# Queue order of a three-branch encoder layer from a timeline simulation

## The chip, the core and the metric

The kernel runs on one core of a Trainium2 chip. The metric is the device time of one execution in microseconds, as the median of several runs. The profile and the trace come from one further execution under the hardware profiler. The engines are TensorE (PE, its weight loads PEld), VectorE (DVE), ScalarE (ACT), GpSimd (POOL) and SyncE (SP), which issues all DMAs of this kernel. Each has a queue of its own that it works off in order, and waits for other engines by semaphores.

## The reference

One layer (DEPTH = 1) on x of shape (1, 1024, 1024) in float32. All three branches read the same modulated, normalised input through one wide projection. The inner functions are only named here; each is a loop over 1024 tokens or over chunks of them.

```python
mod = silu(c) @ ada_w + ada_b                       # shift, scale, gate
h = rmsnorm(x, pre_g) * (1.0 + scale) + shift
proj = h @ w_in                                     # 1024 -> 10496 columns
a_x, a_z, b_u, b_z, c_u, c_z, g_all = split_cols(proj, ...)
y_a = mlstm_branch(a_x, a_z, ...)                   # chunked matrix memory, both directions
filt = hyena_filter(feats, t, ...)
y_b = hyena_branch(b_u, b_z, ..., filt, hy_bias)    # gated long convolution by FFT
y_c = rwkv_branch(c_u, c_z, ...)                    # 16 heads, delta rule, both directions
g_a, g_b, g_c = split(sigmoid(g_all), 3)
merged = g_a * (y_a @ w_branch_a) + g_b * (y_b @ w_branch_b) + g_c * (y_c @ w_branch_c)
x = x + gate * rmsnorm(merged @ w_out, post_g)
```

## The kernel before

Everything is float32. A projection keeps float32 accuracy by splitting both operands into a high and a low part, so each product of a 128 x 128 weight block with 512 tokens is three matmuls (gemm, L343 to L356: high by high L351, low by high L352, high by low L353) that accumulate over eight blocks in a PSUM tile pg, of which there are three. Weights come by load_w (L327 to L335): a DMA into wraw (3 buffers), a cast to wh on ScalarE (L333) and the difference wl on GpSimd (L334; 4 buffers each). ScalarE and VectorE take the result out of PSUM, with the three-tap filters of the branches on the way (taps_job, L409), and the stores to DRAM go out on SyncE.

The stages, in the order of Trunk.all (L1278): modulate (L502) makes h; then _mlstm (L574), the filter and the convolution of the Hyena branch (L870 to L1091); then rwkv (L1347), eight pairs of heads one after the other; then merge (L1142), which ends with the output projection (L1259), the norm and the residual.

The projections are not a stage of their own. Each is a generator in a list of jobs (add, L359; fill, L362), and the stages call fill between their own steps, so that in program order a few matmuls of the projections stand between the steps of a branch. In the scan this is done by weave (L72): per pair of heads, 64 steps of scan (L1740) with owed projection steps spread evenly over them, and at numbered steps the parts of the neighbouring pairs (L1401 to L1420): load, prep, the triangular solve tphase (L1597, on VectorE for the most part: tm and Tb by the helper tt, L476), bonus and post. head_sums (L1424) are two matmuls with a matrix of ones.

A chunk of the scan (L1754 to L1804) is a chain: matmuls U, copy us on VectorE (L1769), matmuls SA, copies into SV on VectorE (L1775) and ScalarE (L1776), matmuls SN, two sums on VectorE (sn), copies into SV for the next chunk on VectorE (L1800) and ScalarE (L1801). All matmuls of the chain write a PSUM tile pch. in_turn (L391) issues a row of small matmuls as a closed run: the first at L395, the others at L398, each tied behind the one before by issue_after and with the highest priority. beside (L384) ties small side work behind an instruction in the same way.

The kernel is written with a tile context. The code only traces instructions in program order; the queues are made when the context is left. Then the traced program is played on a simulated machine, and whenever an engine can take an instruction, it is given, of those whose inputs are ready in that play, the one with the earliest place in program order. tc.high_priority(n) moves the place n instructions forward (in the scan 400 for tphase), and tc.issue_after(i) fixes that what is traced inside is queued behind i on the same engine. The buffers of the pools are handed out in the same play: an instruction that needs a buffer of a pool with none free counts as not ready. The semaphore waits are put in afterwards, for the order found. So the order of each queue, SyncE's DMA issues among them, depends on the durations and delays that the simulated machine gives to each instruction, but what is computed doesn't.

## Time and profile before

| | |
|---|---|
| median of 3 runs | 2182.08 us (2180.28 to 2186.04) |
| the profiled execution | 2200.05 us, span 2198.3 us |
| DMA moved | 262.19 MB, 169384 packets, mean 119 GB/s |
| HBM read, written | 181.06 MB, 78.12 MB |
| SyncE's issues of weight blocks (wraw from w_in) | 340 of 128 KB, 2.3 us from issue to landing |
| chunks of the scan | 128 (8 pairs of 16) |

Span is the time from the first to the last instruction; what lies around it is in the time of the execution but not in the trace. Busy times are a union over an engine's instructions. A matmul's end is modelled and matmuls overlap in the pipeline, so the time from one start to the next is shorter than the duration shown, and a busy TensorE isn't TensorE at its peak. In the view of waits a row gives the idle time of an engine just before its instruction and the instruction that ended this wait.

### The profile page before, as it was taken

The page shows a single profiled execution, that of the slowest core. Times are in us where ns is not written, and L with a number is a line of the kernel's source. Part 1 is how long each engine was busy: PE and PEld are TensorE (multiplying, and loading weights), DVE is VectorE, ACT ScalarE, POOL GpSimd, SP SyncE. Part 2 cuts the span into 40 slices and gives each one's busy share as a digit, 9 for nine tenths or more (in the row PEclk, how much of TensorE's full clock was granted, in tenths as well). Part 3 has the DMA queues.
Part 4 walks back from the last instruction along what each step waited for, and adds up shares of the span by engine and source line. Part 5 has one row for each costly group of instructions (what it writes and reads, how often), then busy time and mean ns, then how long its engine had stood idle before and what let it go on. Part 6 is the DMA issues. An engine that isn't in the chain of part 4 may idle for free. (4 is left out here: it accounts for less than half of the span.)

```text
span 2198.3 us, 45984 instructions
## 1 busy us (share of the span) xinstructions
PE 1994.0 (91%) x17098; PEld 1509.2 (69%) x17098; DVE 1634.6 (74%) x4754; ACT 1103.2 (50%) x2558; POOL 424.3 (19%) x485
## 2 busy tenths in 40 slices
PE   6999899999989899899989999999898887897998
PEld 4666777787868677666766676666666665675786
DVE  4854999988447947788787888868887888764536
ACT  5557356454242115664665756667466564532221
POOL 2211311122222432311101111111114411010200
PEclk9999999999999999999998999999899998897999
DMA  8211222334465345321322333224143542445623
GB/s 255 70 67 59 78 77 90 112 101 127 143 200 172 119 138 163 124 68 61 130 79 93 117 106 102 92 81 136 52 155 118 187 144 63 159 143 175 196 89 129
DMA packets 169384, 262.19 MB, mean 119 GB/s; under 512 B 17863, under 2 KB 87335, under 8 KB 169160
## 3 DMA queue, kind: packets, MB, share of 16 engines
q1 hardware_dynamic: 169160, 259.25, 36.3%
q8 instruction: 135, 2.21, 0.4%
q14 instruction: 89, 0.73, 0.1%
HBM read 181.06 MB, written 78.12 MB: 118 GB/s over the span
## 5 line engine op out<-in xcount | busy, mean ns | idle before, releaser
L334 POOL TENSOR_TENSOR wl<-wraw,wh 128x256 fp32r<-128x256 f32 x408 | 371.5, 915 | 1488.6 <-ACT wh L333 1464.8
L351 PE MATMUL pg<-hh,wh 128*128 128x512 f32 x1440 | 601.5, 418 | 20.9 <-ACT wh L333 11.8
L352 PE MATMUL pg<-hh,wl 128*128 128x512 f32 x1440 | 594.3, 413 | 16.4 <-POOL wl L334 16.3
L353 PE MATMUL pg<-hl,wh 128*128 128x512 f32 x1440 | 592.4, 412 | 1.9 <-DVE hl L565 1.8
L351 PEld LDWEIGHTS pg<-hh,wh 128*128 128x128 f32 x1440 | 278.7, 194 | 88.9 <-ACT wh L333 15.1
L352 PEld LDWEIGHTS pg<-hh,wl 128*128 128x128 f32 x1440 | 279.3, 194 | 78.0 <-POOL wl L334 22.2
L353 PEld LDWEIGHTS pg<-hl,wh 128*128 128x128 f32 x1440 | 278.1, 193 | 62.0 <-DVE hl L565 2.8
L333 ACT CAST wh<-wraw 128x256 fp32r<-128x256 f32 x408 | 162.7, 404 | 220.6 <-PE pg L353 122.1
L476 DVE TENSOR_TENSOR tm<-Ab,Tb 128x126 f32<-128x126 f32 (+22 forms) x496 | 145.4, 293 | 4.4 <-DMA Tb<-in_tinit 2.7
L476 DVE TENSOR_TENSOR Tb<-Tb,tm 128x126 f32<-128x126 f32 (+22 forms) x496 | 144.2, 291 | 1.9
L473 DVE SCALAR_TENSOR_TENSOR st<-pg,hmu,st 128x511 f32<-128x511 f32 (+1 forms) x130 | 80.9, 636 | 27.9 <-ACT e L424 17.6
L476 DVE TENSOR_TENSOR G<-pgr,gmask 128x512 f32<-128x512 f32 x128 | 85.4, 679 | 17.0 <-PE pgr L398 17.0
L457 ACT ACTIVATE st<-pg 128x512 f32<-128x512 f32 x74 | 44.2, 597 | 99.9 <-PE pg L353 95.0
L1684 ACT COPY G<-ar 64x128 f32<-64x128 f32 x256 | 64.3, 295 | 48.4 <-DVE G L476 46.6
L473 DVE SCALAR_TENSOR_TENSOR st<-st,pg 128x512 f32<-128x512 f32 x80 | 54.3, 679 | 35.7 <-PE pg L353 12.7
L398 PE MATMUL pgr<-ar,bk 64*128 64x128 f32 x896 | 76.9, 287 | 0.0
L141 DVE SCALAR_TENSOR_TENSOR row<-row 64x1 f32<-64x1 f32 x393 | 72.7, 208 | 2.1
L1769 DVE COPY us<-pch 128x128 f32<-128x128 f32 x128 | 36.3, 283 | 45.8 <-PE pch L398 45.5
L395 PEld LDWEIGHTS pch<-SV,G 128*64 128x64 f32 x256 | 25.3, 139 | 65.5 <-ACT SV L1801 52.3
L395 PE MATMUL pch<-SV,G 128*64 128x64 f32 x256 | 43.2, 252 | 27.7 <-ACT SV L1801 26.2
L476 DVE TENSOR_TENSOR dw<-dw,dw 128x512 f32<-128x512 f32 x92 | 67.1, 760 | 0.9
L395 PEld LDWEIGHTS pch<-SV,B 128*64 128x64 f32 x256 | 25.3, 139 | 60.1 <-ACT SV L1776 50.1
(677 smaller groups left out, 4228.4 us busy)
## 6 DMA issues: line engine op xcount, KB each, us to landing
wraw<-in_w_in SPq DMA_DIRECT2D x340, 128.0 KB, 2.3
low<-lora SPq DMA_DIRECT2D x32, 512.0 KB, 4.1
sig<-st SPq DMA_DIRECT2D x48, 256.0 KB, 2.6
st<-sig SPq DMA_DIRECT2D x48, 256.0 KB, 3.5
wraw<-in_w_br SPq DMA_DIRECT2D x68, 128.0 KB, 2.8
adw<-in_ada_w SPq DMA_DIRECT2D x16, 512.0 KB, 7.1
x<-in_x SPq DMA_DIRECT2D x8, 512.0 KB, 6.1
hx<-st SPq DMA_DIRECT2D x16, 256.0 KB, 2.0
```

The lines of the kernel that those rows point to most:

```text
L141: self.ops.append(lambda: self.nc.vector.scalar_tensor_tensor(o, a, s, b, op0=op0, op1=op1))
L333: self.nc.scalar.copy(hi, raw)
L334: self.nc.gpsimd.tensor_tensor(lo, raw, hi.bitcast(F32), op=SUB)
L351: nc.tensor.matmul(p, wh, hh, start=(k == 0), stop=False)
L352: nc.tensor.matmul(p, wl, hh, start=False, stop=False)
L353: nc.tensor.matmul(p, wh, hl, start=False, stop=(k == n - 1))
L395: ins = f()
L398: ins = f()
L457: self.nc.scalar.activation(o, p, AF.Tanh, scale=0.5)
L473: return self.nc.vector.scalar_tensor_tensor(out, in0, s, in1, op0=op0, op1=op1)
L476: return self.nc.vector.tensor_tensor(out, a, b, op=op)
L1684: nc.scalar.copy(G[0:64, :, d, h, 0:64], cx["al"][g, d, b % 4][hsl[h]])
```

## The change

One argument of the tile context. The play that orders the queues runs on another simulated machine: before, on the default one, which the scheduler builds for itself; after, on a simulator of the device's timeline, which holds sequencers, queues, engines and DMA as separate resources. Nothing else of the kernel differs: the same instructions are traced, in the same program order, with the same priorities, ties and pools.

```diff
--- before.py
+++ after.py
@@ -1908,7 +1908,7 @@
     A = {n: nc.dram_tensor(f"in_{n}", a.shape, mybir.dt.from_np(a.dtype), kind="ExternalInput").ap()
          for n, a in arrays.items()}
     O = {"out": nc.dram_tensor("out_x", (T, D), F32, kind="ExternalOutput").ap()}
-    with tile.TileContext(nc) as tc:
+    with tile.TileContext(nc, schedule_with_timeline_sim=True) as tc:
         with ExitStack() as ctx:
             Trunk(ctx, tc, A, O).all()
     r = run_bass_kernel_spmd(nc, [{f"in_{n}": a for n, a in arrays.items()}], core_ids=[0])
```

## The prediction, before the result was known

> **What bounds the kernel now.** I read the first lines of the page for the busy shares, then cut the span by stage with the view of windows, then asked the view of waits stage by stage who held TensorE up, and last looked at single places in the timeline.

> ```profile
> span 2198.3 us, 45984 instructions
> PE 1994.0 (91%) x17098; PEld 1509.2 (69%) x17098; DVE 1634.6 (74%) x4754; ACT 1103.2 (50%) x2558; POOL 424.3 (19%) x485
> ...
> core 0: us, PE busy (x) PEld busy (x) DVE busy (x) ACT busy (x) POOL busy (x), PEclk, DMA share, GB/s
> 0.00:110.00 110.00, 85.78 (x459) 58.56 (x460) 72.93 (x295) 56.14 (x96) 25.02 (x27) 0.94 0.55 162
> 110.00:905.00 795.00, 742.72 (x3500) 583.77 (x3498) 597.02 (x1798) 353.41 (x787) 208.18 (x218) 0.97 0.36 118
> 905.00:1985.00 1080.00, 977.73 (x12360) 719.38 (x12360) 858.55 (x2489) 643.34 (x1583) 171.59 (x217) 0.95 0.34 109
> 1985.00:2198.30 213.30, 187.77 (x780) 147.46 (x780) 106.10 (x176) 50.29 (x94) 19.48 (x23) 0.92 0.46 152
> ```

> The four windows are the modulation of x, the mLSTM and Hyena branches, the RWKV scan with its 16 chunks in each of 8 pairs, and the merge. TensorE is the busiest engine in all four. Its idle time is the length less the first number: 24.2, 52.3, 102.3 and 25.5 us, 204.3 in all. Half of it lies in the scan, where VectorE is also busy for 858.55 of 1080 us, so neither engine is full and the time is lost in waiting on each other. Who waits there, for TensorE alone (line, what it waited for, us in total, times, longest):

> ```profile
> PE pch L395 <- ACT SV L1801: 26.2, 25, 5.4
> PE pch L395 <- ACT SV L1776: 21.0, 29, 1.7
> PE pch L395 <- DVE us L1769: 11.7, 20, 2.6
> PE plw L1552 <- DMA low<-lora: 8.3, 8, 1.6
> ```

> The first three rows are the scan's own chain: a chunk's matmuls need a copy (us, SV) that VectorE or ScalarE makes of the matmul before. The projections (the gemm, tile pg) are woven between as filling, and they depend on no chunk. One place shows why TensorE stands still all the same:

> ```profile
> 1833.74 0.39 PE L352 MATMUL pg<-hh,wl 128*128 128x512 f32 x1
> 1835.55 0.27 PE L395 MATMUL pch<-SV,G 128*64 128x64 f32 x1 [1.42 <-ACT SV L1801]
> ...
> 1836.16 0.50 PE L353 MATMUL pg<-hl,wh 128*128 128x512 f32 x1
> ```

> L351 to L353 are three products of one weight block. The third stands behind the chunk's matmul and could have run in the 1.42 us before it: its weights were in use by the matmul before, and when its turn comes it starts with no wait of its own. The queue is in order here, so the place in the queue decides. That is what the change can move; it moves nothing else.

> **What the change does to the work.** It adds and removes no instruction of the kernel: 17098 matmuls, 4754 VectorE and 2558 ScalarE instructions, and every DMA stay, so busy time at a given clock stays. Program order, the edges of issue_after and the offsets of high_priority stay as well, and with them the closed runs of matmuls:

> ```profile
> L398 PE MATMUL pgr<-ar,bk 64*128 64x128 f32 x896 | 76.9, 287 | 0.0
> L1769 DVE COPY us<-pch 128x128 f32<-128x128 f32 x128 | 36.3, 283 | 45.8 <-PE pch L398 45.5
> ```

> The 896 followers of the pgr runs have 0.0 us of idle time ahead of them; they will keep it. What moves is which ready instruction goes first on each of the five queues, SyncE's DMA issues among them, and with it which buffer of a pool frees when. The sum is made on the profiled execution, 2200.05 us (span 2198.3 and 1.75 around it), which is 1.0082 of the median of the three runs, 2182.08; a result of the sum is multiplied by 0.9918.

> Step 1, chain waits in the scan. 26.2 + 21.0 + 11.7 = 58.9 us in 74 waits, 0.80 us each. Undisturbed, the same shape of matmul starts every 87.30/384 = 0.227 us:

> ```profile
> 2102.20:2189.50 87.30, 87.30 (x384) 71.37 (x382) 44.59 (x87) 18.97 (x35) 0.00 (x0) 1.00 0.32 106
> 1854.50:1878.40 23.90, 18.21 (x276) 14.12 (x274) 17.49 (x67) 8.70 (x19) 0.72 (x1) 0.50 0.13 45
> ```

> So a mean wait holds three matmuls of the filling. An order drawn from a timeline that places the copies where the chip has them puts the filling ahead. Not all of it can be had: in the second row TensorE is idle for 5.7 of 23.9 us at the end of a pair, where few projections are left beside the chain. Bounds: 0 and 58.9; I take half, 29 us off.

> Step 2, the rest of the scan's idle time, 102.3 - 58.9 = 43.4 us: loads of low from DRAM, head sums, and many gaps of a pipeline. A DMA that is issued earlier on SyncE would take the 8.3 us row away, the pipeline's gaps stay. Bounds 0 and half; I take a quarter, 11 us off.

> Step 3, weights in the second window. A block is loaded, cast by ScalarE and split by GpSimd, and where these come late TensorE waits:

> ```profile
> PE pg L352 <- POOL wl L334: 16.0, 11, 6.6
> PE pg L351 <- ACT wh L333: 10.2, 5, 5.5
> SPq L330 <- POOL wl L334: 352.2, 136, 17.7
> ```

> That is 26.2 us of the 52.3. The last row (SyncE's own waits, in the scan) shows why it may go either way: a load of wraw waits for the split of an older block to free its buffer, and all DMA issues behind it on SyncE wait with it. Bounds: all 26.2 gained, or as much lost; I take 13 us off, because ScalarE has over half of its time free there (353 of 795 us busy) and only its order delays the cast.

> Step 4, head and end. In the first window the wait is for x to be loaded and scaled, and an order can hardly shorten that; in the end the 384 matmuls of the row above run without a gap. I take 0, with a few us each way.

> ```profile
> PE pxt L544 <- DVE x L540: 15.7, 2, 14.3
> ```

> Step 5, new waits. Every order draws some of its own. The nearest row is ScalarE's, in the scan:

> ```profile
> ACT wh L333 <- PE pg L353: 34.7, 30, 3.3
> ACT SV L1776 <- DVE SV L1775: 51.0, 45, 3.9
> ```

> The cast of the next weights stands ahead of chain copies and waits for a matmul to give its buffer up; 30 times it blocks the whole ScalarE queue. An order that starts casts earlier makes more of these. Bounds 0 and 34.7; I take 15 us, just under half, since ScalarE is free for 40% of the scan and part of it is covered.

> Sum: -29 - 11 - 13 + 15 = -38; 2200.05 - 38 = 2162, times 0.9918 = **2144 us**.

> The granted clock belongs to this, too:

> ```profile
> core 0: 2198.3 us, clock 0.956
> ...
> 1170.00:1175.30 5.30, 2.92 (x62) 2.06 (x63) 5.16 (x22) 1.91 (x5) 0.00 (x0) 1.00 0.01 3
> 1175.30:1188.90 13.60, 13.08 (x186) 10.18 (x178) 9.57 (x24) 6.33 (x11) 0.00 (x0) 0.50 0.36 127
> ```

> A stretch with TensorE busy for 2.92 of 5.30 us is followed by 13.6 us at clock 0.50 in which TensorE is busy throughout. At full clock the same work takes about half, so the thin stretch cost some 6.5 us more than its gaps. Over the span (1 - 0.956) x 2198.3 / 0.5 = 193 us ran at half clock. I put no gain down for it; fewer gaps would give some back, and worse ones take more (rival below). [...]

> ```profile
> 1172.75 0.50 PE L1433 MATMUL phs<-hsp,ones_r 128*128 128x512 f32 x1 [1.18 <-DVE hsp L476]
> ```

> [...]

> **Rivals.** A, slower: the new order lets ready side work go ahead of the chain. In the scan VectorE carries, beside the chain, the triangular solve:

> ```profile
> L476 DVE TENSOR_TENSOR tm<-Ab,Tb 128x126 f32<-128x126 f32 (+22 forms) x496 | 145.4, 293 | 4.4 <-DMA Tb<-in_tinit 2.7
> L476 DVE TENSOR_TENSOR Tb<-Tb,tm 128x126 f32<-128x126 f32 (+22 forms) x496 | 144.2, 291 | 1.9
> ```

> One more pair of these ahead of one chain copy in each of the 128 chunks is (293 + 291) ns x 128 = 75 us, if it isn't covered. It decides once the chain's delay is longer than what TensorE has spare, 102.3/128 = 0.80 us in a chunk of 8.44 us, since the filling is then used up earlier and the last chunks run bare, as at 1854. It gives 2275 x 0.9918 = 2256 us, half of it 2219. For it: VectorE is busy at 79% and its other work is long and mostly ready, and the waits of step 1 show that the chain has no place to spare. Against it: the chain is early in program order, and that goes first among what is ready in either order.

> B, slower by the clock: the filling is used up in bunches and each of the 8 pairs gets one more thin stretch such as that at 1170. It costs 8 x 6.5 = 52 us, 2252 x 0.9918 = 2234 us. It decides where TensorE falls to about half busy for some 5 us. For it: this happens already with 193 us at half clock. Against it: the weaving of the filling is in program order and is not touched.

> C, nothing to be measured: program order and the pinned runs leave so little choice that both orders come out alike, or the argument draws an order that differs where nobody waits. Steps 1 to 5 cancel: 2176 to 2189 us. Against it: 74 chain waits and 30 blocked casts are places where a small shift of the model flips an order.

> **Numbers.** A change under 0.3% (6.5 us) can hardly be told from none here. The forecast has 0.47, rival A 0.28, B 0.10, C 0.15, of which 0.11 lies within 0.3% and 0.04 is a little slower. So faster 0.47, same 0.11, slower 0.28 + 0.10 + 0.04 = 0.42. The forecast's own range goes from every step at its good end (58.9 + 21.7 + 26.2 = 107 us off, 2093 x 0.9918 = 2076 us) to 2175 us, where it meets no change (2182.08 - 6.5); with the rivals the range is 2076 to 2260 us, just above A. Since both signs hold much of the chance, the predicted time is that of the likeliest case, 2144 us.

> **What would show it.** Right: TensorE's idle time in the scan falls from 102 to about 65 us, the three chain rows together to about 30 us, the two rows of weights to about 13, VectorE's busy time stays within a few us of 1634.6, and the span falls by about as much as TensorE's idle time does. Rival A: the chain rows grow, ScalarE's and VectorE's waits for pch shrink (they have other work in hand) and the scan is longer than 1080 us. Rival B: the mean clock falls below 0.956 and the half-clock time grows by 50 us with equal chain rows. The prediction is wrong if the scan gets longer, if the loss is in the second window (weights or DMA issues that come later), or if the busy time of an engine changes by much more than the clock explains.

## The result, and the profile after

The changed kernel takes 2546.7 us (median of four runs; one of them, of 3392.31 us, was disturbed and is left out of the comparison, the others are 2539.41 to 2551.59), the kernel before 2184.06 us beside it: a ratio of 1.164, 95% interval 1.156 to 1.171. It is 16% slower, and above the whole predicted range. The profiled execution of the changed kernel takes 2551.59 us, with a span of 2549.8.

First the busy shares, at the top of the page of the changed kernel:

```profile
span 2549.8 us, 46031 instructions
PE   6999698999999988788699676886689666666898
PEclk9999799999999999799689656797599565666999
```

The second and third line cut the span in 40 slices: how busy TensorE was, and which clock it was granted, both in tenths. Up to the scan (slice 16) both are, taken together, as good as before. In the scan both sink together. The number of matmuls is the same 17098 and VectorE is busy for 1659.4 us (1634.6 before), so no work was added. The windows by stage follow, cut where the first and last copy us stand, of the kernel before and of the changed one. The columns are length, busy time of PE, PEld, DVE, ACT, POOL, granted clock, DMA share, GB/s:

```profile
0.00:929.50 929.50, 850.60 (x4186) 658.76 (x4188) 684.40 (x2120) 429.35 (x914) 235.13 (x247) 0.97 0.38 123
929.50:1983.60 1054.10, 954.51 (x12118) 702.01 (x12118) 843.59 (x2457) 623.27 (x1550) 169.66 (x215) 0.95 0.34 109
1983.60:2198.30 214.70, 188.90 (x798) 148.40 (x796) 106.60 (x178) 50.55 (x95) 19.48 (x23) 0.91 0.46 151
```

```profile
0.00:1024.60 1024.60, 938.79 (x4591) 742.89 (x4593) 717.55 (x2150) 452.68 (x972) 248.40 (x283) 0.96 0.38 121
1024.60:2340.40 1315.80, 1002.97 (x11713) 776.02 (x11713) 835.28 (x2427) 607.61 (x1489) 126.22 (x179) 0.74 0.25 80
2340.40:2549.80 209.40, 185.14 (x798) 146.70 (x796) 106.54 (x178) 49.67 (x95) 20.46 (x23) 0.93 0.46 155
```

Of 351.5 us more span, 95.1 lie before the scan, 261.7 in it, and the end is 5.3 shorter. The 95.1 us look like work: TensorE is busy 88.2 us longer and executes 405 matmuls more (4591 against 4186). All 405 are projection matmuls (3045 against 2640), which at the 0.227 us of the prediction are 92 us. That this is the cause isn't shown: rest_old, below, is as long there without them. The 405 are missing from the scan (11713 against 12118), which is longer all the same: TensorE's idle time there went from 99.6 to 312.8 us and its clock from 0.95 to 0.74.

The waits of the changed kernel in the scan, TensorE's first (the chain's three rows, and two of the rest):

```profile
PE pch L395 <- ACT SV L1801: 63.2, 38, 4.5
PE pch L395 <- ACT SV L1776: 47.7, 43, 5.8
PE pch L395 <- DVE us L1769: 31.9, 36, 3.9
PE ptv L1693 <- DVE G L476: 28.8, 43, 1.4
PE plw L1552 <- DMA low<-lora: 23.0, 21, 2.4
```

VectorE's, of the changed kernel and then of the kernel before:

```profile
DVE us L1769 <- PE pch L398: 93.6, 46, 8.6
DVE SV L1775 <- PE pch L398: 82.2, 39, 6.0
DVE sn L476 <- PE pch L398: 73.9, 44, 6.2
```

```profile
DVE us L1769 <- PE pch L398: 43.1, 44, 3.5
DVE sn L476 <- PE pch L398: 37.5, 48, 4.3
DVE SV L1775 <- PE pch L398: 24.5, 32, 2.4
```

And ScalarE's, of the changed kernel:

```profile
ACT SV L1776 <- DVE SV L1775: 132.7, 59, 6.3
ACT G L1684 <- DVE G L476: 106.3, 48, 6.2
ACT SV L1801 <- DVE sn L476: 94.1, 59, 5.5
ACT wh L333 <- PE pg L353: 52.7, 43, 7.3
```

The three chain rows of TensorE are 142.8 us, 58.9 before. VectorE waits for the chain's matmuls for 249.7 us with waits of up to 8.6 us; that was 105.1 us (43.1 + 37.5 + 24.5) with a longest of 4.3. TensorE is late for VectorE, and VectorE for TensorE. The timeline of the changed kernel's first pair shows what TensorE does while VectorE waits:

```profile
1110.05 0.27 PE L395 MATMUL pch<-us,tt 64*64 64x64 f32 x1
...
1110.67 0.50 PE L353 MATMUL pg<-hl,wh 128*128 128x512 f32 x1
1111.00 0.39 PE L351 MATMUL pg<-hh,wh 128*128 128x512 f32 x1
...
1116.07 0.40 PE L353 MATMUL pg<-hl,wh 128*128 128x512 f32 x1
1116.40 0.27 PE L395 MATMUL pch<-SV,B 128*64 128x64 f32 x1
...
1116.78 0.50 PE L351 MATMUL pg<-hh,wh 128*128 128x512 f32 x1
...
1121.97 0.63 PE L352 MATMUL pg<-hh,wl 128*128 128x512 f32 x2
1122.52 0.27 PE L395 MATMUL pch<-SV,G 128*64 128x64 f32 x1
```

The three pch matmuls begin three legs that follow each other in the chain: SA and SN of one chunk and U of the next. Between them stand whole blocks of projection matmuls, with two matmuls of the head sums in each, back to back, some 5.7 us each, and the legs start at once when they follow: none has a wait in brackets. Both copies into SV that the leg at 1116.40 needs were done by 1111.13 (on ScalarE 0.26 us from 1110.87), so it was kept 5.3 us by the queue and by nothing else. Counted over the scan by their lines L351 to L353, projection matmuls stood in 410 unbroken runs before, median 3, longest 19, 13% of them in runs of 12 or more. Now they stand in 91 runs, median 15, longest 24, 89% in runs of 12 or more.

By pairs of heads: before, every pair took 126 to 156 us (the last 99) with 136 to 257 projection matmuls in it. Now four pairs with 257 to 336 of them take 172 to 201 us, one with 103 takes 162, two with none take 139 and 144, and the last, with none either, takes 103. So the filling is used up in bunches, and neither the full nor the bare pairs are fast.

### The profile page after: what moved, and what is told of

Read it like the earlier page. It is cut to its first block, busy times and chain, and to the rows that moved or that the text cites. A ratio compares the mean times of both kernels' runs of the same rounds, so it can differ in the third digit from the quotient of the medians.

```text
span 2549.8 us, 46031 instructions
## 1 busy us (share of the span) xinstructions
PE 2126.9 (83%) x17098; PEld 1665.6 (65%) x17098; DVE 1659.4 (65%) x4754; ACT 1110.0 (44%) x2556; POOL 395.1 (15%) x485
## 5 line engine op out<-in xcount | busy, mean ns | idle before, releaser
L351 PE MATMUL pg<-hh,wh 128*128 128x512 f32 x1440 | 578.0, 408 | 37.2 <-DVE st L473 18.5
L352 PE MATMUL pg<-hh,wl 128*128 128x512 f32 x1440 | 576.2, 402 | 1.2 <-POOL wl L334 1.1
L353 PE MATMUL pg<-hl,wh 128*128 128x512 f32 x1440 | 575.7, 402 | 0.8 <-POOL hl L1108 0.4
L334 POOL TENSOR_TENSOR wl<-wraw,wh 128x256 fp32r<-128x256 f32 x408 | 343.7, 847 | 1273.0 <-ACT wh L333 1250.3
L351 PEld LDWEIGHTS pg<-hh,wh 128*128 128x128 f32 x1440 | 276.2, 192 | 109.2 <-issue 18.0
L353 PEld LDWEIGHTS pg<-hl,wh 128*128 128x128 f32 x1440 | 275.9, 192 | 67.9 <-issue 5.8
L352 PEld LDWEIGHTS pg<-hh,wl 128*128 128x128 f32 x1440 | 276.8, 192 | 63.0 <-POOL wl L334 3.5
L333 ACT CAST wh<-wraw 128x256 fp32r<-128x256 f32 x408 | 162.1, 403 | 273.1 <-PE pg L353 188.6
L476 DVE TENSOR_TENSOR tm<-Ab,Tb 128x126 f32<-128x126 f32 (+22 forms) x496 | 135.0, 272 | 8.4
L476 DVE TENSOR_TENSOR Tb<-Tb,tm 128x126 f32<-128x126 f32 (+22 forms) x496 | 134.5, 271 | 9.2
L395 PE MATMUL pch<-SV,G 128*64 128x64 f32 x256 | 51.8, 296 | 63.6 <-ACT SV L1801 63.2
L398 PE MATMUL pgr<-ar,bk 64*128 64x128 f32 x896 | 99.8, 345 | 0.0
L1769 DVE COPY us<-pch 128x128 f32<-128x128 f32 x128 | 36.5, 285 | 93.8 <-PE pch L398 93.6
L1776 ACT COPY SV<-pch 64x128 f32<-64x128 f32 x128 | 33.5, 262 | 142.2 <-DVE SV L1775 134.9
L395 PEld LDWEIGHTS pch<-SV,G 128*64 128x64 f32 x256 | 31.2, 173 | 96.3 <-ACT SV L1801 82.2
L395 PE MATMUL pch<-SV,B 128*64 128x64 f32 x256 | 52.8, 301 | 48.0 <-ACT SV L1776 48.0
L1775 DVE COPY SV<-pch 64x128 f32<-64x128 f32 x128 | 35.3, 276 | 83.1 <-PE pch L398 83.0
L476 DVE TENSOR_TENSOR G<-pgr,gmask 128x512 f32<-128x512 f32 x128 | 82.5, 682 | 8.9 <-PE pgr L398 7.9
```

The source lines that it names most:

```text
L333: self.nc.scalar.copy(hi, raw)
L334: self.nc.gpsimd.tensor_tensor(lo, raw, hi.bitcast(F32), op=SUB)
L351: nc.tensor.matmul(p, wh, hh, start=(k == 0), stop=False)
L352: nc.tensor.matmul(p, wl, hh, start=False, stop=False)
L353: nc.tensor.matmul(p, wh, hl, start=False, stop=(k == n - 1))
L395: ins = f()
```

## The experiments

Theory 1: the new order lets ready projection matmuls go ahead on TensorE's queue, so the chain waits behind them, and later pairs run bare. Theory 2: VectorE's and ScalarE's side work goes ahead of the chain (rival A). Theory 3: only the clock is lost (rival B). Five figures were taken from each trace, beside its mean clock: the time to the first copy us; the projection matmuls up to there; the length of the scan; and two sums over the 128 chunks. The first, **late matmuls**, is the time from the end of the copy that a leg needs to the start of its first matmul. The second, **late copies**, goes from the end of a leg's matmuls to the end of the copy or sum made of them, so it holds the copies themselves. The two don't make up the whole scan. Each ratio is against runs of the kernel before on the same chip (medians of 2183.81 to 2189.42 us).

| kernel | median us | ratio (95%) | before the scan us | projection matmuls there | scan us | late matmuls us | late copies us | clock |
|---|---|---|---|---|---|---|---|---|
| before | 2184.06 | | 929.5 | 2640 | 1054 | 176 | 619 | 0.956 |
| after | 2546.7 | 1.164 (1.156 to 1.171) | 1024.6 | 3045 | 1316 | 400 | 664 | 0.846 |
| tie_before | 2265.77 | 1.037 (1.032 to 1.042) | 912.7 | 2532 | 1134 | 253 | 658 | 0.950 |
| tie_after | 2402.56 | 1.099 (1.095 to 1.102) | 982.0 | 2532 | 1191 | 280 | 683 | 0.921 |
| prio_after | 2532.33 | one run | 1022.9 | 3045 | 1300 | 405 | 646 | 0.855 |
| bare_before | 2600.96 | one run | 1330.6 | 4320 | 1053 | 205 | 522 | 0.828 |
| bare_after | 2585.58 | one run | 1050.6 | 3265 | 1323 | 384 | 653 | 0.832 |
| tie1_before | 2262.34 | 1.035 (1.032 to 1.039) | 921.4 | 2532 | 1123 | 242 | 660 | 0.950 |
| tie1_after | 2543.57 | 1.164 (1.160 to 1.169) | 982.2 | 2532 | 1342 | 468 | 667 | 0.891 |
| all_after | 2552.08 | 1.168 (1.163 to 1.173) | 1000.7 | 2532 | 1324 | 455 | 667 | 0.893 |
| pe_old | 2370.45 | 1.086 (1.083 to 1.089) | 934.9 | 2640 | 1222 | 266 | 659 | 0.927 |
| pe_new | 2672.05 | 1.224 (1.220 to 1.228) | 1083.9 | 3045 | 1373 | 655 | 465 | 0.830 |
| rest_old | 2531.68 | one run | 1030.1 | 2640 | 1287 | 405 | 575 | 0.889 |
| pe_dve_old | 2229.53 | 1.021 (1.017 to 1.025) | 927.1 | 2640 | 1086 | 205 | 606 | 0.954 |
| pe_act_old | 2315.56 | 1.061 (1.057 to 1.066) | 935.7 | 2640 | 1163 | 189 | 703 | 0.941 |
| pe_old_g | 2347.42 | 1.074 (1.070 to 1.078) | 934.4 | 2640 | 1200 | 264 | 645 | 0.933 |
| g_before | 2197.42 | 1.006 (1.003 to 1.008) | 924.2 | 2640 | 1062 | 175 | 604 | 0.956 |
| later_before | 2176.04 | 0.994 (0.992 to 0.996) | 917.8 | 2533 | 1041 | 164 | 640 | 0.967 |
| later2_before | 2180.38 | 0.9965 (0.9947 to 0.9983) | 918.9 | 2592 | 1050 | 170 | 617 | 0.958 |
| later3_before | 2190.38 | 1.001 (0.998 to 1.004) | 910.0 | 2485 | 1063 | 197 | 635 | 0.964 |

**The filling tied to the chain.** tie_after and tie_before (new and old simulation): each projection matmul that weave places in the scan is queued behind the last leg traced before it; legs gets the last matmul of each of the three legs of a chunk.

```diff
+    def fill_tied(self, n):
+        with self.tc.issue_after(self.legs[-1].ins) if len(self.legs) > 0 else ExitStack():
+            self.fill(n)
...
-                weave(self.scan(...), at, self.fill, ...)
+                weave(self.scan(...), at, self.fill_tied, ...)
...
+            self.legs.append(ins)
```

> New order, but each projection matmul that is woven into the scan is tied (queue order only) behind the chain matmuls that precede it in program order, so that it can no longer be queued ahead of them. Theory 1 (run-ahead: ready projection matmuls are queued in blocks ahead of the chain, then later pairs run bare at half clock): 2150 to 2260 us, over 170 projection matmuls in every pair but the last, mean clock 0.93 or more. Theory 2 (VectorE's and ScalarE's side work goes ahead of the chain, rival A): stays above 2450 us, because the tie touches TensorE's queue alone.

> The same tie in the old order, as the control. Both theories: little change, 2160 to 2230 us, since the old order has few projection matmuls ahead of the chain; it tells what the tie itself costs or gains.

The old order pays 82 us for the tie, more than expected; the new order gains 144 us of its 363 and ends between the two theories, so neither alone fits. So the filling's place is a cause and not the whole: with the same number of projection matmuls in each pair 137 us stay between the two, 69 before the scan and 57 in it.

**The chain first.** prio_after: the matmuls, copies and sums of each chunk of the scan are given the highest priority, in the new order.

```diff
+            with self.tc.high_priority(10 ** 6):
                 ins = self.in_turn(partial(nc.tensor.matmul, U[hsl[h], d], G[:, j, d, h, 0:64], SV[:, h, at[d]],
...
```

> New order, with every instruction of a chunk's chain (matmuls, copies, sums) at the highest priority. Theory 1: 2480 to 2560 us, since the projection matmuls are queued while the chain's inputs are not yet there, and priority chooses only among what is ready. Theory 2: below 2300 us, since side work then comes after every chain instruction that is ready.

2532 us, one run, and pair by pair within 11 us of the changed kernel. A place further forward in program order moves almost nothing: so it is not that others rank ahead of the chain. That leaves that the chain isn't ready in the play when the queue is given away; the play itself was not looked into.

**No filling in the scan.** bare_after and bare_before: all projections that are left are traced before the scan.

```diff
             prep1 = iter(())
+            self.fill(10 ** 6)
             run(self.setup(cx[0], 0))
```

> New order, with all projections put ahead of the scan in program order, so that the scan has no filling. Theory 1: the scan takes the same time as with the same edit in the old order, within 4%: 8 pairs of about 140 us, total about 929 + 388 + 1090 + 215 = 2620 us. Theory 2: the scan is at least 15% longer than the old order's, 1250 us and more, as the side work is still there.

> The old order with all projections issued before the scan, so that its chunks run without filling. Theory 1 (the loss is TensorE's: ready projection matmuls run ahead in blocks, the chain waits behind them, and later pairs are bare): without filling the two orders hardly differ, so pairs 2 to 8 take 133 to 144 us each at a granted clock of 0.60 to 0.67, as in the new order without filling (133.4 to 143.7), and the total is 2500 to 2600 us. Theory 2 (VectorE and ScalarE carry side work ahead of the chain in the new order): a bare pair of the old order is shorter than that by 8 us or more, 115 to 130 us. Theory 3 (only the clock is lost): the pairs here are as slow as in the new order, which it shares with theory 1.

In the new order the first pair still drew in 1055 of these matmuls and took 378 us, so the scan as a whole (1323 us) says nothing of the two theories; pairs 2 to 7 took 134 to 143 us. In the old order seven pairs took 133 to 139 us: without filling the two orders differ by 3% (means of 140.0 and 136.2 us). What the filling costs in the scan comes out of two rows, of bare_before and of the kernel before (shown above):

```profile
1330.60:2383.60 1053.00, 729.01 (x10432) 568.44 (x10432) 731.88 (x2337) 532.86 (x1314) 8.31 (x36) 0.63 0.18 61
```

1053.0 us with no projection matmul, 1054.1 us with 1680: in the old order the scan takes as long as it does bare, and 1680 matmuls, 381 us by 0.227 us each, cost nothing on balance. On balance, because the bare scan runs at a clock of 0.63 and the filled one at 0.95: what the filling may cost and what it may win back by the clock were not told apart. Done ahead of the scan the 1680 cost their price, 401 us. In the new order the scan with 1275 of them is 263 us longer than the bare one of the old.

**How tight, and where.** tie1_after and tie1_before let a projection matmul go ahead by one leg. all_after also ties, before the scan, each projection matmul behind the ninth last matmul or transpose that its stage has traced (stage_mm).

```diff
-        with self.tc.issue_after(self.legs[-1].ins) if len(self.legs) > 0 else ExitStack():
+        with self.tc.issue_after(self.legs[-2].ins) if len(self.legs) > 1 else ExitStack():
...
+        self.tc.add_manual_dep(ins.ins, self.stage_mm[-9], dep, reason="behind")
```

> The new order, each woven projection matmul tied behind the last but one chain run instead of the last, so it may run ahead by one leg of a chunk (some five matmuls, about 1 us). Theory 1: the chain's delay by run-ahead comes back in part, and the wait that the tight tie adds goes; 2340 to 2430 us, against 2402.6 with the tight tie and 2546.7 with none. Theory 2: run-ahead is not what costs, so a looser tie is as good as the tight one less its own cost of some 80 us: 2300 to 2340 us.

> The same looser tie in the old order. It runs ahead by a median of three matmuls by itself, so the looser tie binds less: 2185 to 2230 us, against 2265.8 with the tight tie, by both theories. Above 2250 us would mean that the tie costs by something other than the place of the filling.

> The new order, looser tie in the scan, and before the scan each projection matmul tied behind the ninth last matmul or transpose that its stage has traced. Theory 1, carried to the stages before the scan (filling run ahead in the first stages is missing in the later ones): the part before the scan falls from 982 us to 910 to 950 us, and the total to 2280 to 2370 us. Theory 2, or a loss by the order of VectorE and ScalarE in these stages: the part before the scan stays at 970 to 1000 us.

All three missed. One leg of freedom was enough for the new order to lose all that the tight tie had won; the late matmuls rose from 280 to 468 us with about as many projection matmuls in each pair, 203 to 217. So evenness by pair isn't enough; the mean wait of the matmuls SA alone went from 325 to 1994 ns, so it counts which leg a run of filling stands ahead of. tie1_before shows that the tie's own price is not its tightness. And the part before the scan didn't get shorter with all_after, which fell as a remedy; that tie wasn't run in the old order, so what it costs by itself isn't known.

**One queue at a time.** The order of each queue was read off the two built programs, and instructions pinned in it, each behind the one before it; ORDERS holds the indices of the traced instructions, one list for each pinned queue. pe_old: new simulation, TensorE's queue pinned in the old order. pe_new: old simulation, TensorE's queue pinned in the new order. rest_old: new simulation, the other four queues pinned in the old order.

```diff
+def pin(nc, tc):
+    traced = list(nc.cur_bb.bb.instructions)
+    for order in ORDERS:
+        for i, j in zip(order, order[1:]):
+            tc.add_manual_dep(traced[j], traced[i].name, dep, reason="pin")
...
             Trunk(ctx, tc, A, O).all()
+            pin(nc, tc)
```

> The new simulation with one queue taken out of its hands: TensorE's 11528 instructions are pinned, each behind the one before it, in the order that the kernel before has; VectorE, ScalarE, GpSimd and SyncE are ordered by the new simulation around it. Theory 1 (the loss is the place of the projection matmuls on TensorE's queue, before the scan as well as in it): 2150 to 2230 us, the part before the scan 920 to 950, the scan 1040 to 1090 us. Theory 2 (the other four queues, ScalarE's and VectorE's above all, carry the loss, or a part such as the 137 us that stayed between the two tied kernels): over 2300 us. Theory 3 (the clock alone) follows theory 1 here: with the old placement of matmuls the clock is 0.94 to 0.96.

> The counterpart: the old simulation, with TensorE's queue alone pinned in the order of the changed kernel. Theory 1: 2480 to 2600 us, pairs of some 200 us first and bare ones of 140 us last, clock 0.83 to 0.87. Theory 2: the four other queues are ordered by the old simulation, so most of the loss is gone, below 2350 us.

> The new simulation for TensorE alone: the queues of VectorE, ScalarE, GpSimd and SyncE are pinned in the order of the kernel before. Theory 1 in its simplest form (the new simulation draws the filling ahead whenever it is ready): 2350 to 2550 us. If what bounds the run-ahead is when ScalarE's casts and evictions and SyncE's weight loads stand in their queues, the old order of these holds the filling back: 2190 to 2300 us. Theory 2: as the kernel before, 2170 to 2210 us.

The rows of pe_old and of rest_old for the part before the scan and the scan:

```profile
0.00:934.90 934.90, 849.19 (x4186) 662.39 (x4186) 694.79 (x2120) 435.23 (x921) 227.38 (x251) 0.97 0.38 124
934.90:2156.80 1221.90, 1008.53 (x12118) 743.65 (x12118) 865.52 (x2456) 625.12 (x1543) 165.11 (x211) 0.90 0.29 94
```

```profile
0.00:1030.10 1030.10, 898.31 (x4186) 688.63 (x4186) 684.32 (x2120) 420.33 (x917) 230.74 (x247) 0.93 0.34 111
1030.10:2316.70 1286.60, 1033.67 (x12118) 786.68 (x12118) 839.60 (x2457) 620.43 (x1547) 169.74 (x215) 0.85 0.27 89
```

pe_old misses what theory 1 said and lies where theory 2 put it (over 2300 us); rest_old, a single run, lies within theory 1's range, and pe_new above it. Before the scan it is TensorE's queue: 934.9 us with the old one, though the others are new, and 1024.6 to 1083.9 with a new one. In rest_old the 100.6 us more of that part are 52.9 us of idle time of TensorE and 47.7 us of busy time, at a clock of 0.93 where it was 0.97. In the scan TensorE's queue alone (rest_old) costs 233 us, and most of them lie in the late matmuls, 229 us more, while the late copies fall by 44. But theory 1 isn't all: with TensorE in the old order, the other four still cost 168 us in the scan, which theory 1 had at 36 at most. Without filling this hardly shows: the bare pairs of bare_after, with all five queues new, were within 3% of those of the old order. The two don't add up (233 + 168 against 262 in the changed kernel); pe_new is slower than the changed kernel, perhaps since its other queues were not drawn around the same blocks; that wasn't tested.

**Which of the others.** The late copies of pe_old, in its timeline:

```profile
1409.98 0.52 PE L398 MATMUL pch<-us,tt 64*64 64x64 f32 x5
...
1410.33 1.27 DVE L473 SCALAR_TENSOR_TENSOR kk<-k,nkk,kk 128x1024 f32<-128x1024 f32 x1
...
1411.65 1.28 DVE L476 TENSOR_TENSOR G<-pgr,gmask 128x512 f32<-128x512 f32 x2
...
1412.85 0.74 DVE L473 SCALAR_TENSOR_TENSOR P<-P,hlgb,tmp 128x512 f32<-128x512 f32 x1
1413.51 0.74 DVE L473 SCALAR_TENSOR_TENSOR s<-s,hlgb,a 128x512 f32<-128x512 f32 x1
1414.17 0.27 DVE L1775 COPY SV<-pch 64x128 f32<-64x128 f32 x1
```

The leg's matmuls ended at 1410.50; the copy SV of 0.27 us starts 3.67 us later, behind five long products for other chunks and pairs. This is what rival A foresaw, side work ahead of a chain copy on VectorE, though none of the five is of the triangular solve. Over the scan, G stands ahead of a ready SV on VectorE for 28.1 us (6.9 before). pe_dve_old and pe_act_old pin TensorE and one more queue in the old order; pe_old_g pins TensorE, and on VectorE and ScalarE only the chain's copies and sums and the G products among themselves. The edits are the pin above with other lists.

> The new simulation with TensorE's and VectorE's queues pinned in the old order; ScalarE, GpSimd and SyncE are ordered by the new one. With TensorE alone pinned it was 2370.45 us, 186 above the kernel before. Theory 4 (side work on VectorE goes ahead of the chain's copies, rival A of the prediction, and ScalarE only follows since its work waits for VectorE's): 2190 to 2250 us. Theory 5 (ScalarE carries the most: its copies G, casts and B stand ahead of its half of SV): 2290 to 2360 us.

> The same with TensorE's and ScalarE's queues pinned in the old order and VectorE, GpSimd and SyncE ordered by the new simulation. Theory 4: VectorE's order still costs, 2290 to 2360 us. Theory 5: 2190 to 2250 us. If both kernels lie near 2190 to 2250 us, the loss needs both queues to differ (one pulls the other's order with it); if both lie at 2300 us or more, each carries a loss of its own or GpSimd and SyncE do.

> TensorE's queue in the old order, and among themselves the chain's copies and sums (us, SV, sn) and the products and copies that make G for the next chunks keep the old order on VectorE and ScalarE; everything else on these and the other queues is ordered by the new simulation. If G ahead of the copies into SV is the cost (28.1 against 6.9 us on VectorE, 37.0 against 16.9 us on ScalarE): 21 to 41 us less than 2370, so 2325 to 2350 us. If the loss is spread over all side work: 2360 to 2375 us. Below 2300 us: G was the root and more hung on it.

The scan of pe_dve_old, and of pe_act_old:

```profile
927.10:2012.60 1085.50, 960.08 (x12118) 706.89 (x12118) 838.00 (x2457) 620.70 (x1543) 168.87 (x211) 0.94 0.32 106
```

```profile
935.70:2099.10 1163.40, 987.38 (x12118) 727.14 (x12118) 867.37 (x2457) 623.73 (x1551) 168.77 (x215) 0.92 0.30 99
```

It is VectorE for the most part, as theory 4 had it: its old order takes 141 of the 186 us back, ScalarE's alone 55. In pe_act_old the late matmuls are down to 189 us (176 before) and the late copies up to 703 (619). With both TensorE and VectorE old, 2.1% (1.7 to 2.5) is left for ScalarE, GpSimd and SyncE, which were not told apart. G is a part of it, 23 us, at the low end of what was expected. Where the rest lies is open. Counted in the traces, between the end of a leg's matmuls and the start of the copy or sum made of them, VectorE ran G for 18 us in the kernel before and for 42 in pe_old, st (which takes projections out of PSUM) for 9 and 21, but tm and Tb of the triangular solve for 76 and 81, hardly more.

**Two ideas for the old order.** g_before ties G behind the copies into SV. later_before, later2_before and later3_before trace fewer projection steps before the scan (in the mLSTM branch, in the Hyena convolution, in both), which leaves more for the scan.

```diff
-                self.fill(8)
+                self.fill(4)
...
-            self.fill(8)
+            self.fill(4)
...
-            self.fill(16)
+            self.fill(8)
...
-            self.fill(12)
+            self.fill(8)
...
-NP, ND = 3, 2
+NP, ND = 2, 2
```

The first four are later_before, the last later2_before; for g_before, where svc holds the last copies into SV and what follows makes G:

```diff
+        with ExitStack() as after:
+            for ins in self.svc or ():
+                after.enter_context(self.tc.issue_after(ins.ins))
...
```

> The kernel before, old simulation, with the products and copies that make G tied behind the last copies into SV on their engines, so they never stand ahead of these. If the 6.9 us on VectorE and 16.9 us on ScalarE in which G stood ahead of a ready copy come back: 2165 to 2180 us. If G is then late for the next chunk's matmuls, or the tie draws the rest of the order another way: 2190 to 2230 us.

> The kernel before with fewer projection steps owed in the mLSTM branch (four fills of 8 steps to 4, and one each of 8 to 4, 16 to 8 and 12 to 8): 32 steps of 6 matmuls, 192 matmuls or 44 us of TensorE, go to later places, the scan in the end. If what is done before the scan is paid and the scan carries it for nothing: 2140 to 2175 us. If the later stages take them up, or the mLSTM branch then stands without cover: 2180 to 2200 us. If the scan has no room for more: 2200 us or more.

> The kernel before with NP 2 in place of 3, the projection steps behind each product of the Hyena convolution. The same question at another place, where DMA is busiest: 2150 to 2180 us if the scan carries what is moved for nothing, 2180 to 2200 us if the convolution waits for its own chain instead, above that if the scan has no room.

> Both edits together (fewer fills in the mLSTM branch, NP 2 in the convolution), old simulation. If the scan still carries what is moved for nothing, the gains add: a ratio near 0.990, 2160 to 2172 us. If its room ends, or the convolution stands without cover: 2172 to 2190 us.

g_before is 0.6% slower; late copies fell by 15 us, and the scan grew by 8 all the same. later_before is 0.6% faster than the kernel before (0.4 to 0.8) and the fastest kernel of the study: of the 192 matmuls 107 left the part before the scan, the rest went to later stages of it; it is 11.7 us shorter (24 us by their price). Of the 107, 49 run in the scan, which is 12.7 us shorter all the same, and 58 behind its last copy us; each figure is from one profiled execution. later2_before gives 0.35%, both together nothing (1.001, 0.998 to 1.004): that part is 19.5 us shorter then and the scan 8.5 longer. The first two lie just above the range in which the scan carries what is moved for nothing, the third just above both its ranges. So the scan carries a little more for nothing, and its room ends soon, as far as differences of under 1% can show it.

## Why the prediction was wrong

**What moves.** "What moves is which ready instruction goes first" holds, and the parts that stay did stay: the 896 followers have 0.0 us of idle time ahead of them, and the counts are the same (but for two records of ScalarE, 2556 for 2558).

```profile
L398 PE MATMUL pgr<-ar,bk 64*128 64x128 f32 x896 | 99.8, 345 | 0.0
```

**Step 1 failed**, and with it the sign. It took for given that an order drawn from a timeline fills a gap of 0.80 us with the three projection matmuls that it holds and no more. The order put them ahead, as forecast, but a median of 15 in a row where 3 stood. The bound "0 and 58.9 us gained" left out that filling which goes first is a price for the chain. The three rows grew by 83.9 us, and the late matmuls by 224. rest_old shows the cause by itself, in one run: TensorE's queue from the new simulation, all others old, +233 us in the scan.

**Step 2** (the rest of the scan's idle time, -11) failed too: it grew from 41 us (99.6 - 58.9 in this cut) to 170 (312.8 - 142.8). The wait for low, which an earlier DMA was to take away, rose from 8.3 to 23.0 us, and ptv, which waits for VectorE's G, from 2.4 to 28.8.

**Step 3** (weights, -13) was right on the two rows and wrong on what they are worth: the 26.2 us are down to 0.2 among TensorE's waits from 110 us to the scan, and SyncE's wait for the split fell from 352.2 to 167.5 us in the scan. But TensorE's idle time before the scan didn't fall; it went from 78.9 to 85.8 us (929.50 - 850.60 and 1024.60 - 938.79), as other waits came in their place:

```profile
PE pcl L728 <- ACT X L716: 14.8, 1, 14.8
PE pg L351 <- DVE st L473: 11.6, 4, 7.0
...
SPq L330 <- POOL wl L334: 167.5, 97, 12.4
```

**Step 4** (head and end, 0) was right: the wait for x is 14.1 us for 15.7, the end 209.4 us for 214.7.

```profile
PE pxt L544 <- DVE x L540: 14.1, 1, 14.1
```

**Step 5** (new waits, +15) named casts on ScalarE. These grew from 34.7 to 52.7 us, by 18, close to the sum's 15, though a wait on ScalarE isn't yet time of the kernel; the new waits that decide are on TensorE and VectorE, for the chain, and were not in the sum at all.

**Rival A** had the direction and half of the mechanism. VectorE's order goes with most of the 128 us that pe_act_old takes more than the kernel before beside it (2315.56 against 2187.77), with TensorE and ScalarE in the old order: the late copies rise by 84 us. It forecast 75, and that this is near is luck: it counted one more pair of tm and Tb for each chunk, and in pe_act_old these stand there for 78 us where 76 were, while G went from 18 to 42 and st from 9 to 22 (counted as above). It also left out that TensorE's own filling is side work of the same kind, and in the scan the larger share (233 us alone against 168 for the other four). Its test, that VectorE's waits for pch shrink, came out the other way (105 to 250 us), because of TensorE: with its queue alone new (rest_old) the same three rows are 304 us. And what spoke against it, "the chain is early in program order", fell with prio_after.

**Rival B** had the clock, not the cause: 0.956 to 0.846, or 785 us at half clock ((1 - 0.846) x 2549.8 / 0.5) where 193 were. "The weaving of the filling is in program order and is not touched" fell: program order fixes from where a filling matmul may be taken, not when. But a low clock alone doesn't make the scan as long as the changed kernel's: bare_before has a clock of 0.63 there and takes no longer than the kernel before with 0.95. And the clock came back with the order: 0.954 in pe_dve_old. How much of the loss goes through the clock stays open, since no run changed one without the other, and how much shorter a bare pair would be at full clock was not tried.

**Rival C** failed: the play has far more choice than the closed runs suggested.

Two things more stay open: why the new simulation draws the filling ahead in blocks, since its play and its durations were not looked into, and what in TensorE's queue makes the stages before the scan longer with rest_old, which has the same 2640 projection matmuls there as the kernel before.

## What to carry to other kernels

Filling beside a chain was free here while it stood in small pieces between the chain's legs: 1680 matmuls cost nothing in one order, and with 1275 of them in blocks, 289 us by 0.227 us each, the scan was 263 us longer in the other, from the same program. When a tool is to order the queues anew, put a bound below zero on every step that "fills the gap", and ask what the filled engine's next dependent has to wait for. To find the queue that carries a loss, pin the others in the order that was good, one after another: six runs told here what ties and priorities had not.

## What the runs showed of the hardware

In a bare pair of the changed kernel the clock stays at half for 51.2 us in one piece:

```profile
1429.11:1480.31 51.20, 36.30 (x470) 27.56 (x472) 34.54 (x97) 29.39 (x71) 0.34 (x3) 0.50 0.24 78
```

In the thin stretch of the prediction, 1170.00 to 1175.30 in the kernel before, the longest gap of TensorE is the 1.18 us of the row at 1172.75, and the clock of the 13.6 us behind it is 0.50. What makes the clock fall or come back was not shown.

The two sums of time at half clock, 193 and 785 us, take the clock to be 1.00 or 0.50. In windows of 0.5 us it reads one of the two in 4343 of 4396 in the kernel before and in 4998 of 5099 in the changed one. At 0.50, projection matmuls of the kernel before start 0.43 us apart (four from 1187.19 to 1188.47, shown with 0.62 to 0.63 us each); at 1.00 it is the 0.227 us of the prediction.
